# The last block of two down projections as seven quarter products, in a two-layer transformer kernel

## The chip, the core and the metric

The kernel runs on one core of a Trainium2 chip. The time is the device time of the program in microseconds (us). The kernel before took 988.21 us, the median of three runs (988.11 to 988.47).

## What is computed

Two transformer layers on 512 tokens of width 1024, in fp32. Layer A mixes tokens with latent attention, layer B with banded attention; behind each stands an MLP with a squared relu, and behind each mixer and each MLP a layer norm:

```python
def _layernorm(x, g, b):
    mu = x.mean(-1, keepdims=True)
    var = jnp.square(x - mu).mean(-1, keepdims=True)
    return (x - mu) * lax.rsqrt(var + LN_EPS) * g + b

def _mlp(x, w_up, w_down):                 # w_up 1024x4096, w_down 4096x1024
    h = jax.nn.relu(x @ w_up)
    return (h * h) @ w_down

# each layer, alpha = sqrt(2):
x = _layernorm(alpha * x + mixer(x), ln_mix_g[l], ln_mix_b[l])
x = _layernorm(alpha * x + _mlp(x, w_up[l], w_down[l]), ln_mlp_g[l], ln_mlp_b[l])
```

## The kernel before

**Products of split numbers.** TensorE (PE) multiplies in a reduced fp32 form, so each operand is split into a high and a low part (`split`, lines 72 to 84: ScalarE, called ACT here, writes the high part on L77; VectorE, called DVE, subtracts it from the source on L81, or GpSimd, called POOL, if the caller says so). A product is three matmuls: high by high, high by low, low by high (`three`, `group`, L105). Weights come by DMA in pieces of 128x1024 (512 KB), are split into tiles `wh` and `wl` (four of each in rotation), and a weight piece is prepared at most four pieces ahead (`weights`, `AHEAD`).

**Seven products for eight.** Hidden width 4096 is worked in four blocks of 1024 (q = 0 to 3). A block of the up projection, and of the down projection, is a product of two matrices cut into 2x2 quarters, and it is made with seven quarter products in place of eight (the scheme of Winograd). They are named U1 to U7 and D1 to D7. The left factors are sums of quarters: D1 takes a11, D2 a12, D4 a22, D5 a21 - a22, D6 a21 - a22 - a11, D3 a12 plus that sum, D7 a11 - a21 (`Factors.sum`, L700 to L708: DVE, 128x1024 each); each factor is then split (`factor`; tiles `fac`, three in rotation). The right factors are sums of weight quarters, and the DMA makes them: after a weight piece has been split for one product, `add_more` (L204) adds another quarter into the same tile `wq` by a DMA on POOL's queue, and the next product splits the sum. Tile `quada` goes through D1, D5, D6 and D4 in this way, `quadb` through D3 and D7; D2 loads its own quarter (`raw`). Each quarter product takes two weight pieces and, for each of two token tiles (t = 0, 1), 12 matmuls of 128x512 into one PSUM bank. So a D step is 24 matmuls.

**The order.** `STEPS` (line 39) is a table of numbers: one row of it per block, in which U' and D' belong to the next block. PE's instructions keep this written order; a scheduler places those of the other engines, ahead of which a few pins (`pe`, `pin`) and "not before" marks (`behind`) stand. Every engine works through its own list in order and waits where an input is missing. `down_` adds each product from its bank to the residual rows x in SBUF with DVE (L638, L641, L792); products D1 and D6 gather in `u2` (L900).

**The last block before.** In the row for q = 2 to 3 stands `LAST_STEPS`: it ends with U'6 U'7 U'4 D4, and the down projection of block q = 3 is not in it. That block is a plain product (`TokMajor`, class `Hidden`): the four quarters of the hidden rows are split as they are, and eight weight pieces are loaded and split. `finish` first makes columns 0 to 511 for all four token tiles (piece by piece), and then columns 512 to 1023 token by token: 24 matmuls for a token, `add_last` (add and statistics, L631), then `layer_norm(t)` (statistics L488, the power on POOL L443, two DVE passes over 128x1024, L494 and L495), while PE goes on with the next token. In layer A the finished rows of tokens t = 0 and 1 are turned over on PE (`turn_tokens`, L507: 8 transposes into the two banks `tr`, split by ACT and DVE into `xth` and `xtl`) behind the matmuls of tokens 1 and 2; tokens 2 and 3 are turned within `begin`, the start of layer B, between its first products. In layer B the last token's columns 512 to 1023 are made in two halves, and `last_norm` ends the kernel: bank `b` gets x times g less the mean by PE with `xg` (L466, L472, L477) for the lower columns, DVE does the rest (L479, L481), and each piece goes out by its own DMA (L482).

**Layer B's mixer.** For heads h = 0 to 15, `scores`, `weigh`, `turn` and `mix` run with fixed leads. POOL scales the weights of a head (`p`, L1451), masks them (`pm`, L1471), splits some weights of w_sq and w_so (L81), and splits the mixed rows of each of the eight head pairs into `oh` and `ol` (in `mix`); that last split stands behind `muls[h + 4]`, the scaling of a later head. `run_steps` interleaves `proj.part`, the products with w_so, which need `oh` and `ol`.

Of the kernel before, what the change touches and what calls it, by code (L numbers as in the profile page):

```python
# [9 lines left out]
F32R = mybir.dt.float32r  # L10
# [5 lines left out]
P = 128  # L16
# [23 lines left out]
FIRST_STEPS, LAST_STEPS = "U'1 U'2 U'5 U'3 U'6 U'7 U'4 D'1 D'2", "U'1 D5 U'2 D3 U'5 D6 D7 U'3 U'6 U'7 U'4 D4"  # L40
# [8 lines left out]
def build(tc, nc, io, out):  # L49
    with ExitStack() as top:  # L50
# [117 lines left out]
        def queue_seven(name, key, chunk):  # L168
# [20 lines left out]
            def grown(a, jp, *more, aside=None):  # L189
                wh, wl = tiles_of_weights(aside)  # L190
                after = None
                if aside and not early:
                    after = state.pop("plain", None)
                elif (key, a, jp, bool(more)) == ("U", "b", 0, True):
                    after = state.get("s4")
                elif (key, a, more) == ("U", "a", (1, 0)):
                    after = state.pop(("s2", jp), None)
                with behind(after):
                    state["last"] = split(
                        wh, wl, flat(half(a, jp)), keep=(a, bool(more)) == ("b", True) and key == "U"  # L200
                    )
# [29 lines left out]
            def alone(jp, aside=None):  # L231
# [3 lines left out]
                with behind(state["plain"] if aside else state.pop("f1", None) if key == "D" else None):  # L235
                    split(wh, wl, raw)
# [12 lines left out]
            def add(n, asides=(None, None)):  # L249
                for jp, aside in enumerate(asides):  # L250
                    make = (lambda jp=jp, aside=aside: of[n](jp, aside)) if aside else (lambda jp=jp: of[n](jp))
                    stream.append((name, make))
                    off_ring.append(aside is not None)
# [4 lines left out]
        def steps_of():  # L258

            rows = [(-1, FIRST_STEPS)] + [(q, STEPS) for q in range(NFF - 2)] + [(NFF - 2, LAST_STEPS)]  # L260
# [23 lines left out]
        def mlp_stream(l):  # L284
# [13 lines left out]
            add |= {("D", q): queue_seven("down", "D", down(q)) for q in range(NFF - 1)}  # L298
# [6 lines left out]
            for c in range(8):  # L305
                queue("down", io["down"][l, (NFF - 1) * 8 + c])
# [153 lines left out]
        def last_tokens(gb):  # L460
# [8 lines left out]
        def last_norm(gb, minus, diag, xg, b):  # L469

            x = xs[NT - 1]
            pe(nc.tensor.matmul(b, ident, xg, start=True, stop=False))  # L472
            mv = sp.tile([P, 2], F32, tag="mv", bufs=4, name=nm("mv"))
            nc.vector.bn_aggr(mv, stats[NT - 1])
            r = rsqrt_of(mv[:, 1:2])
            nc.scalar.activation(diag, minus, AF.Copy, scale=mv[:, 0:1])
            pe(nc.tensor.matmul(b, diag, gb[0][:, 0:512], start=False, stop=True))  # L477
            late = slice(512, D)
            nc.vector.scalar_tensor_tensor(x[:, late], x[:, late], mv[:, 0:1], gb[0][:, late], ALU.subtract, ALU.mult)  # L479
            for c, src in ((late, x[:, late]), (slice(0, 256), b[:, 0:256]), (slice(256, 512), b[:, 256:512])):  # L480
                pin(nc.vector.scalar_tensor_tensor(x[:, c], src, r, gb[1][:, c], ALU.mult, ALU.add))  # L481
                nc.sync.dma_start(out[(NT - 1) * P : NT * P, c], x[:, c])  # L482

        def layer_norm(t, gb, dst):
# [9 lines left out]
            pin(nc.vector.scalar_tensor_tensor(x, x, mv[:, 0:1], gb[0], ALU.subtract, ALU.mult))  # L494
# [26 lines left out]
        class TokMajor:  # L521
# [25 lines left out]
            def finish(self, gb=None, dst=None, early=None, gb_at=None):  # L547
# [9 lines left out]
                if gb is not None:  # L557
# [3 lines left out]
                    for t in range(NT):  # L561
                        end = dst is None and t == NT - 1
                        n = 2 if end else 1
                        if end:
                            parts = last_tokens(gb)
                        for i in range(n):
                            c = slice(i * 512 // n, (i + 1) * 512 // n)
                            b = bank(512 // n)
                            for kp in range(4):
                                self.group(b, t, kp, ws[kp], c)  # L570
                            pinned[0] = early
                            with tc.high_priority():
                                self.evac(t, slice(512 + c.start, 512 + c.stop), b)
                            pinned[0] = False
                        pinned[0] = early
                        with tc.high_priority():
                            if end:
                                last_norm(gb, *parts)
                            else:
                                layer_norm(t, gb, dst)  # L580
                        if early:
                            prepare(early[t])
                        pinned[0] = False
                        if dst is not None and t in (1, 2):
# [40 lines left out]
        def count(t, c):  # L625
# [4 lines left out]
            for i in range(c.start // n, c.stop // n):  # L630
                pin(nc.vector.bn_stats(stats[t][:, i, :], xs[t][:, i * n : (i + 1) * n]))  # L631
# [144 lines left out]
        def mlp(src, gb, dst, mp):  # L776
# [17 lines left out]
            class Block:  # L794
                def __init__(self, q):
# [4 lines left out]
                    self.fac = {}  # L800

# [69 lines left out]
                def factor(self, n, quad=False):  # L871
                    if quad:
                        f = mp.tile([P, 2, 4, 256], F32R, tag="quada", bufs=1, name=nm("fac"))
                    else:
                        f = mp.tile([P, 2, 4, 256], F32R, tag="fac", bufs=3, name=nm("fac"))
                    g = [self.g.get(a) for a in ("a11", "a12", "a21", "a22")]
                    pair = split(f[:, 0], f[:, 1], g[2] if n == 0 else self.down.sum(n, *g))
                    if (self.q, n) == (0, 1):
                        state["f1"] = state["first"] = pair
                    self.fac[n] = f  # L880

                def down_(self, n):
                    w = [weights("down") for _ in range(2)]
                    f = self.fac.pop(n)
                    key = {3: 5}.get(n) or own_bank[n]
                    for t in range(2):
                        tk = slice(t * P, (t + 1) * P)
                        b = self.bank(("D", key), t)
                        for m in range(4):
                            wh, wl = w[m // 2]  # L890
                            c = slice(m % 2 * 512, (m % 2 + 1) * 512)
                            group(
                                b, three(f[:, 0, m, tk], f[:, 1, m, tk], wh[:, c], wl[:, c]),
                                n not in (2, 3, 4) and m == 0, m == 3, skip_group_check=True,
                            )
                        add = add_scaled if self.q == 0 else add_plain
                        if n == 1 and self.q == 0:
                            nc.vector.tensor_copy(u2[t], b)
                        elif n in (1, 6):
                            nc.vector.tensor_add(u2[t], b, u2[t])  # L900
                        elif n == 2:
                            add(t, lows, b)
                        elif n == 5:
                            add(2 + t, highs, b)
                        elif n == 3:
                            add(t, highs, b)
                        elif n == 7:
                            take(2 + t, highs, b)
                        elif n == 4:
                            add(2 + t, lows, b)  # L910
# [5 lines left out]
            for i, (which, q, n) in enumerate(steps):  # L916
                if which == "D":

                    i_q = steps.index(("U", q, {1: 6, 2: 2}.get(n, 4)))
                    i_last = steps.index(("U", q + 1, {2: 2, 3: 2}.get(n, 6))) - 1  # L920

                    at.setdefault(i_q if (q, n) == (0, 1) else max(min(i - 2, i_last), i_q), []).append((q, n))
            for i, (which, q, n) in enumerate(steps):
                if which == "U":
                    blocks[q].up(n)
                else:
                    blocks[q].down_(n)
                    if (q, n) == (NFF - 2, 6):
                        for t in range(2):
                            take(t, highs, u2[t])  # L930
# [734 lines left out]
```

## Time and profile before

| what | value |
|---|---|
| median of three runs | 988.21 us |
| the profiled execution, its own time | 988.92 us |
| its span, first to last instruction | 987.1 us |
| DVE, ACT, POOL busy | 771.0, 545.5, 240.1 us |
| granted clock of TensorE | 1.00 |
| read from HBM, written | 146.41 MB, 4.22 MB |

A row of the timeline gives start and duration in us, engine, source line, operation, output and inputs, shape and count, and in brackets how long the engine had idled before and who released it. A duration reaches over the start of the next instruction where the engine works in a pipeline, so what an instruction costs its engine is the distance from its start to the next one's. PEld is the loading of weights into TensorE, which lies beside the matmuls.

### The profile page before, as it was taken

What the parts mean: (1) busy time and instruction counts of PE and PEld (TensorE: products, weight loads), DVE (VectorE), ACT (ScalarE), POOL (GpSimd) and SP (SyncE); (2) the same over time, 40 slices, a digit from 0 to 9 for tenths busy, and PEclk for the clock granted to TensorE, in tenths of its full rate; (3) what the DMA queues carried; (4) which work ended last, traced back from release to release, by engine and by line L of the source; (5) the groups of instructions that cost most, each with busy time, mean ns of one, the idle gap of its engine ahead of it and who ended that gap; (6) DMA issues with size and microseconds to landing.
All of it is one profiled execution on the core that took longest, in us unless ns stands there. A gap on an engine that the chain in (4) does not pass through costs nothing.

```text
span 987.1 us, 15665 instructions
## 1 busy us (share of the span) xinstructions
PE 979.5 (99%) x6028; PEld 881.6 (89%) x6028; DVE 771.0 (78%) x1279; ACT 545.5 (55%) x842; POOL 240.1 (24%) x207
## 2 busy tenths in 40 slices
PE   9999999999999999999999999999999999999998
PEld 9988888998999999998898988789998998999986
DVE  6589967989778769887587788798885986888756
ACT  5557644467537637646136787436763763764620
POOL 0231101121212211310002898522221122023000
PEclk9999999999999999999999999999999999999999
DMA  7421236389879968973232212628997797898332
GB/s 263 146 89 43 87 128 193 64 215 234 149 177 234 185 133 245 221 128 120 93 108 86 97 65 97 192 44 173 259 183 126 237 201 119 222 261 146 82 128 85
DMA packets 60678, 149.54 MB, mean 151 GB/s; under 512 B 5259, under 2 KB 10300, under 8 KB 60604
## 3 DMA queue, kind: packets, MB, share of 16 engines
q0 software_dynamic: 24320, 58.73, 34.0%
q1 hardware_dynamic: 36140, 89.56, 26.2%
q8 instruction: 47, 0.77, 0.3%
q10 hardware_dynamic: 144, 0.26, 0.1%
q14 instruction: 27, 0.22, 0.1%
HBM read 146.41 MB, written 4.22 MB: 153 GB/s over the span
## 4 chain that ended last, share of the span: by engine, by line
PE 96%; DVE 2%; POOL 1%; ACT 0%; issue 0%; DVEq 0%; POOLq 0%
PE mm L105 88%; PE tr L105 5%; PE tr L1243 1%; PE tr L742 1%; POOL wl L81 1%; DVE mm L1431 0%; PE tr L1467 0%; DVE o L1502 0%; PE tr L507 0%; POOL p L1451 0%; DVE pt L81 0%; POOL ol L81 0%; PE tr L1007 0%; ACT wh L77 0%; DVE mm L1427 0%
## 5 line engine op out<-in xcount | busy, mean ns | idle before, releaser
L105 PE MATMUL mm<-wh,fac 128*128 128x512 f32 (+1 forms) x944 | 292.7, 386 | 0.0
L77 ACT ACTIVATE wh<-wq 128x1024 fp32r<-128x1024 f32 x164 | 173.9, 1062 | 184.3 <-PE mm L105 137.0
L81 DVE TENSOR_TENSOR wl<-wq,wh 128x1024 fp32r<-128x1024 f32 x164 | 199.4, 1221 | 68.3 <-ACT wh L77 67.5
L105 PE MATMUL mm<-xth,wh 128*128 128x256 f32 (+1 forms) x928 | 243.4, 290 | 0.0
L105 PE MATMUL mm<-xth,wl 128*128 128x256 f32 (+1 forms) x800 | 233.3, 292 | 0.0
L105 PEld LDWEIGHTS mm<-wh,fac 128*128 128x128 f32 x944 | 176.2, 188 | 35.5 <-DVE fac L81 0.6
L105 PE MATMUL mm<-xtl,wh 128*128 128x256 f32 (+1 forms) x672 | 197.1, 293 | 0.0
L105 PE MATMUL mm<-wl,fac 128*128 128x512 f32 (+1 forms) x472 | 182.3, 386 | 0.0
L105 PEld LDWEIGHTS mm<-xth,wh 128*128 128x128 f32 x928 | 168.6, 192 | 3.1
L105 PEld LDWEIGHTS mm<-xth,wl 128*128 128x128 f32 x800 | 153.2, 192 | 2.7
L105 PEld LDWEIGHTS mm<-xtl,wh 128*128 128x128 f32 x672 | 128.7, 191 | 3.0
L77 ACT ACTIVATE wh<-raw 128x1024 fp32r<-128x1024 f32 (+3 forms) x86 | 85.0, 990 | 78.1 <-PE mm L105 57.1
L204 POOL DMA_DIRECT2D wq<-in_up x64 | 77.6, 1238 | 200.2 <-DVE wl L81 193.0
L105 PEld LDWEIGHTS mm<-wl,fac 128*128 128x128 f32 x472 | 88.8, 188 | 16.6
L81 DVE TENSOR_TENSOR wl<-raw,wh 128x1024 fp32r<-128x1024 f32 (+2 forms) x64 | 74.8, 1178 | 30.8 <-ACT wh L77 30.5
L204 POOL DMA_DIRECT2D wq<-in_down x48 | 42.0, 875 | 189.1 <-DVE wl L81 183.2
L81 POOL TENSOR_TENSOR wl<-raw,wh 128x1024 fp32r<-128x1024 f32 (+2 forms) x22 | 47.0, 2138 | 90.3 <-ACT wh L77 70.3
L105 PE MATMUL mm<-wh,ol 128*128 128x512 f32 x128 | 50.3, 393 | 0.9 <-POOL ol L81 0.9
L105 PE MATMUL mm<-wh,oh 128*128 128x512 f32 x128 | 50.7, 396 | 0.0
L105 PE MATMUL mm<-wl,oh 128*128 128x512 f32 x128 | 50.1, 391 | 0.1
L443 POOL TENSOR_TENSOR rs<-mv,half 128x1 f32<-128x1 f32 x16 | 8.9, 554 | 168.1 <-DVE mv L488 163.3
L641 DVE TENSOR_TENSOR x<-mm,x 128x512 f32<-128x512 f32 (+1 forms) x49 | 32.9, 675 | 14.8 <-PE mm L105 14.8
(246 smaller groups left out, 1788.5 us busy)
## 6 DMA issues: line engine op xcount, KB each, us to landing
wq<-in_up POOLq DMA_DIRECT2D x64, 512.0 KB, 7.3
wq<-in_down POOLq DMA_DIRECT2D x48, 512.0 KB, 7.3
wq<-in_up SPq DMA_DIRECT2D x32, 512.0 KB, 6.6
raw<-in_down SPq DMA_DIRECT2D x28, 512.0 KB, 6.1
wq<-in_down SPq DMA_DIRECT2D x24, 512.0 KB, 5.5
raw<-in_up SPq DMA_DIRECT2D x16, 512.0 KB, 4.7
raw<-in_w_o SPq DMA_DIRECT2D x8, 512.0 KB, 3.3
raw<-in_w_sq SPq DMA_DIRECT2D x8, 512.0 KB, 3.3
```

Source lines behind the costliest of these rows:

```text
L77: high = nc.scalar.activation(dst_h, src, AF.Copy)
L81: low = (engine or nc.vector).tensor_sub(dst_l, src, f32(dst_h))
L105: pe(nc.tensor.matmul(dst, st, mv, start=first and i == 0, stop=last and i == len(pairs) - 1, **kw))
L204: state["added", key, a, more, jp] = nc.gpsimd.dma_start(half(a, jp), chunk(*more, jp), accum_op=ALU.add)
L443: state["rs"] = nc.gpsimd.tensor_tensor(r, v, half, ALU.pow)
L641: nc.vector.tensor_add(xs[t][:, c], b, xs[t][:, c])
L742: pe(nc.tensor.transpose(pt[:, a, :], xs[t][:, k * P : (k + 1) * P], ident))
L1243: pe(nc.tensor.transpose(pt[:, kb * P : (kb + 1) * P], p[:, kb * P : (kb + 1) * P], ident))
```

## The change

Block q = 3 of both down projections gets the seven products too. `STEPS` now also serves the row from q = 2 to 3 (so D4 of block 2 stands ahead of U'6, and D'1 D'2 follow U'4), and a last row "D5 D3 D6 D7 D4" follows. `TokMajor` and class `Hidden` are no longer used there, the eight plain weight pieces are no longer loaded, and `u2` is no longer taken apart at the end of block 2.

What becomes of the products of the last block stands in a new function, `last_out`. D1 adds to `u2`; D2 adds to x (columns 0 to 511, with statistics), and then ACT writes `u2` into D2's bank, on which D6 and then D7 go on summing; D5 and D3 go to x as before. D6 completes columns 512 to 1023 of tokens 0 and 1: DVE takes the bank from x, and `layer_norm` of these tokens stands right there. Behind D7, `u2` and D7 go to tokens 2 and 3, and ACT copies columns 0 to 511 of these tokens into new banks, on which D4 sums. So these columns are never written back to x before the norm: `layer_norm` reads them from the bank (`lows`). D4's two weight pieces get their low parts from POOL. Weight splits of this block stand behind the splits of factors (`state["last", ...]`).

In layer A tokens 0 and 1 are turned behind D7 and between the two halves of D4. In layer B D4 of token 3 is made in two banks of 256 columns; token 2's second pass of the norm is a scale on ACT and additions on POOL and DVE (`state["rest"]`), and `last_norm` is laid out over DVE, ACT and POOL, with six output DMAs in place of four behind token 1.

In layer B's mixer, ACT's eviction `low` of the second bank stands behind the sink exponential of a later head; the split of the mixed rows of head pairs m = 5, 6 and 7 goes to DVE, and only m < 5 waits for `muls[h + 4]`.

**DVE, layer A, the end of the last block.** `x_1598`, `x_1600`, `x_1602` and `x_1604` are the rows of tokens 0 to 3; `mm_4826` and `mm_4840` are the banks of D6 and D7, `fac_5043` is D4's factor. Before, where the norm of token 0 is made (`mm_4988` and `mm_5021` are tokens' own banks):

```order
L641 TENSOR_TENSOR x_1598<-mm_4988,x_1598 128x512
L631 BN_STATS bn_4936<-x_1598 128x6
L488 BN_AGGR mv_5015<-bn_4936 128x2
L494 SCALAR_TENSOR_TENSOR x_1598<-x_1598,mv_5015,gb_4890 128x1024
L495 SCALAR_TENSOR_TENSOR x_1598<-x_1598,rs_5017,gb_4890 128x1024
L641 TENSOR_TENSOR x_1600<-mm_5021,x_1600 128x512
L631 BN_STATS bn_4946<-x_1600 128x6
L81 TENSOR_TENSOR xtl_1829<-tr_5054,xth_1827 128x4x128
```

Now, in the same place:

```order
L81 TENSOR_TENSOR wl_4996<-wq_4864,wh_4995 128x1024
L81 TENSOR_TENSOR fac_5043<-a_778_4783,fac_5043 128x1024
L804 TENSOR_TENSOR x_1598<-x_1598,mm_4826 128x512
L804 TENSOR_TENSOR x_1600<-x_1600,mm_4840 128x512
L642 BN_STATS bn_4884<-x_1598 128x6
L642 BN_STATS bn_4901<-x_1600 128x6
L505 BN_AGGR mv_5017<-bn_4884 128x2
L505 BN_AGGR mv_5037<-bn_4901 128x2
L512 SCALAR_TENSOR_TENSOR x_1598<-x_1598,mv_5017,gb_4905 128x1024
L512 SCALAR_TENSOR_TENSOR x_1600<-x_1600,mv_5037,gb_4905 128x1024
L653 TENSOR_TENSOR x_1602<-mm_4826,x_1602 128x512
L804 TENSOR_TENSOR x_1602<-x_1602,mm_4826 128x512
```

The norms of tokens 0 and 1 now stand together, behind the splits for D7 and D4 and ahead of the additions of D7.

**PE, layer A, the turning of token 0.** Before, the last row of token 1's products, the transposes, and the first of token 2's (`fac_4820`):

```order
L105 MATMUL mm_5021<-wl_4972,fac_4817 128x512
L105 MATMUL mm_5021<-wh_4971,fac_4817 128x512
L507 MATMUL tr_5054<-ident,x_1598 128x128 x4
L507 MATMUL tr_5061<-ident,x_1598 128x128 x4
L105 MATMUL mm_5068<-wh_4861,fac_4820 128x512
```

Now D7's last rows (`fac_4991`), the transposes, and D4's first (`fac_5043`):

```order
L105 MATMUL mm_4840<-wl_4996,fac_4991 128x512
L105 MATMUL mm_4840<-wh_4995,fac_4991 128x512
L530 MATMUL tr_5093<-ident,x_1598 128x128 x4
L530 MATMUL tr_5100<-ident,x_1598 128x128 x4
L105 MATMUL mm_5069<-wh_4999,fac_5043 128x512
```

The transposes of token 0 were one token's products (24 matmuls) behind its last sum; now they follow D7 at once, and D4 stands behind them.

**POOL, the end of layer A's MLP.** Before, after the last additions to up weights, the four powers of the norms:

```order
L204 DMA wq_4083<-in_up 128x2x512 x2
L443 TENSOR_TENSOR rs_5017<-mv_5015,half 128x1
L443 TENSOR_TENSOR rs_5050<-mv_5048,half 128x1
L443 TENSOR_TENSOR rs_5097<-mv_5095,half 128x1
L443 TENSOR_TENSOR rs_5145<-mv_5143,half 128x1
```

Now (`wl_5000` and `wl_5047` are the low parts of D4's weights):

```order
L209 DMA wq_4083<-in_up 128x2x512 x2
L209 DMA wq_4682<-in_down 128x1024 x4
L209 DMA wq_4864<-in_down 128x1024 x2
L209 DMA wq_4682<-in_down 128x1024 x2
L81 TENSOR_TENSOR wl_5000<-wq_4682,wh_4999 128x1024
L81 TENSOR_TENSOR wl_5047<-wq_4682,wh_5046 128x1024
L449 TENSOR_TENSOR rs_5019<-mv_5017,half 128x1
L449 TENSOR_TENSOR rs_5039<-mv_5037,half 128x1
```

Eight adding DMAs and two splits of 128x1024 now stand ahead of the first power.

The diff, cut to its core:

```diff
-FIRST_STEPS, LAST_STEPS = "U'1 U'2 U'5 U'3 U'6 U'7 U'4 D'1 D'2", "U'1 D5 U'2 D3 U'5 D6 D7 U'3 U'6 U'7 U'4 D4"
+FIRST_STEPS, LAST_STEPS = "U'1 U'2 U'5 U'3 U'6 U'7 U'4 D'1 D'2", "D5 D3 D6 D7 D4"
...
+                if last:
+                    after = state.pop(("last", state["product"], jp), None)
+                    if state["product"] == 4:
+                        low = nc.gpsimd
...
-            for c in range(8):
-                queue("down", io["down"][l, (NFF - 1) * 8 + c])
...
-            nc.gpsimd.tensor_mul(xg, xs[NT - 1][:, 0:512], gb[0][:, 0:512])
-            return minus, diag, xg, bank()
+            nc.gpsimd.tensor_mul(xg, xs[NT - 1][:, 512:D], gb[0][:, 512:D])
+            return minus, diag, xg, [bank(256) for _ in range(2)]
...
+            t, before, b1 = state["rest"]
+            for c, engine in ((slice(0, 512), nc.gpsimd), (slice(512, D), nc.vector)):
+                engine.tensor_add(before[:, c], before[:, c], b1[:, c])
+                nc.sync.dma_start(out[t * P : (t + 1) * P, c], before[:, c])
             nc.scalar.activation(diag, minus, AF.Copy, scale=mv[:, 0:1])
...
+            for c, to in zip((early, late), b):
+                pe(nc.tensor.matmul(to, diag, gb[0][:, c], start=False, stop=True))
+            for i, src in enumerate(lows):
+                c = slice(i * 256, i * 256 + 256)
+                pin(nc.vector.scalar_tensor_tensor(x[:, c], src[:, 0:256], mv[:, 0:1], gb[0][:, c], ALU.subtract, ALU.mult))
+            nc.scalar.activation(x[:, early], b[0], AF.Copy, scale=r)
+            nc.gpsimd.tensor_add(x[:, early], x[:, early], gb[1][:, early])
+            for c, src in ((lows_, x[:, lows_]), (late, b[1])):
                 pin(nc.vector.scalar_tensor_tensor(x[:, c], src, r, gb[1][:, c], ALU.mult, ALU.add))
                 nc.sync.dma_start(out[(NT - 1) * P : NT * P, c], x[:, c])
+            nc.scalar.dma_start(out[(NT - 1) * P : NT * P, early], x[:, early])
...
+                def last_out(self, n, t, b):
+                    if n == 1:
+                        nc.vector.tensor_add(u2[t], b, u2[t])
+                    elif n == 2:
+                        add_last(t, lows, b)
+                        nc.scalar.activation(b, u2[t], AF.Copy)
...
+                    elif n == 6:
+                        with tc.high_priority():
+                            take(t, highs, b)
+                            count(t, highs)
+                            layer_norm(t, self.gb, dst)
+                    elif n == 7:
+                        add_plain(2 + t, lows, b)
+                        n_banks = 2 if dst is None and t == 1 else 1
+                        self.seeded[t] = bs = [bank() for _ in range(n_banks)]
+                        for i, to in enumerate(bs):
+                            cols = slice(i * 512 // n_banks, (i + 1) * 512 // n_banks)
+                            nc.scalar.activation(to[:, 0 : cols.stop - cols.start], xs[2 + t][:, cols], AF.Copy)
+                        take(2 + t, highs, b)
+                        count(2 + t, highs)
+                        if dst is not None and t == 1:
+                            with tc.high_priority():
+                                dst.turn(0)
+                    elif n == 4:
...
+                            layer_norm(2 + t, self.gb, dst, b)
+                            if dst is not None and t == 0:
+                                dst.turn(1)
...
-            TokMajor(Hidden(), add_last, "down").finish(gb, dst, dst and (0, 0, 0, 1), 1)
...
-                    nc.scalar.activation(low, parts[hi], AF.Copy)
+                    with behind((sinks[min(h + 4, SQH - 1)],) if n2 else None):
+                        nc.scalar.activation(low, parts[hi], AF.Copy)
...
-                state["open"] = (muls[min(h + 4, SQH - 1)],)
-                split(oh[m // 4][:, m % 4, :], ol[m // 4][:, m % 4, :], o.rearrange("p a b -> p (a b)"), nc.gpsimd)
+                if m < 5:
+                    state["open"] = (muls[h + 4],)
+                split(oh[m // 4][:, m % 4, :], ol[m // 4][:, m % 4, :], o.rearrange("p a b -> p (a b)"), nc.gpsimd if m < 5 else None)
```

More of the change, by code (lines that the diff above doesn't have):

```diff
@@ L561, in finish @@
                     for t in range(NT):
[L562 to L575, printed above, removed]
-                        with tc.high_priority():
[L577 to L582, printed above, removed]
+                        b = bank()
+                        for kp in range(4):
+                            self.group(b, t, kp, ws[kp])
+                        pinned[0] = True
+                        with tc.high_priority():
+                            self.evac(t, slice(512, D), b)
+                        with tc.high_priority():
+                            layer_norm(t, gb, dst)
+                        prepare(early[t])
                         pinned[0] = False
-                        if dst is not None and t in (1, 2):
+                        if t in (1, 2):
                             with tc.high_priority():
@@ L868, in up_out, with factor @@
                             nc.scalar.activation(self.g[done], self.g[done], AF.Square)
[L871 to L875, printed above, removed]
+                def factor(self, n):
+                    f = mp.tile([P, 2, 4, 256], F32R, tag="fac", bufs=3, name=nm("fac"))
                     g = [self.g.get(a) for a in ("a11", "a12", "a21", "a22")]
-                    pair = split(f[:, 0], f[:, 1], g[2] if n == 0 else self.down.sum(n, *g))
+                    pair = split(f[:, 0], f[:, 1], self.down.sum(n, *g))
                     if (self.q, n) == (0, 1):
                         state["f1"] = state["first"] = pair
+                    if self.q == NFF - 1:
+                        if n == 3:
+                            state["fac3"] = pair
+                        for jp in range(2):
+                            state["last", {5: 3, 3: 6, 6: 7, 7: 4}.get(n), jp] = pair
                     self.fac[n] = f
@@ L884, in down_ @@
                     f = self.fac.pop(n)
-                    key = {3: 5}.get(n) or own_bank[n]
+                    last = self.q == NFF - 1
+                    key = {3: 5}.get(n) or (1 if last and n in (6, 7) else own_bank[n])
+                    seeded = n in (2, 3, 4) or last and n in (6, 7)
                     for t in range(2):
                         tk = slice(t * P, (t + 1) * P)
[L888 to L910, printed above, removed]
@@ new lines, in down_ @@
+                        bs = self.seeded[t] if last and n == 4 else [self.bank(("D", key), t)]
+                        if len(bs) > 1:
+                            parts = last_tokens(self.gb)
+                        for i, b in enumerate(bs):
+                            cols = slice(i * 512 // len(bs), (i + 1) * 512 // len(bs))
+                            for m in range(4):
+                                wh, wl = w[m // 2]
+                                c = slice(m % 2 * 512 + cols.start, m % 2 * 512 + cols.stop)
+                                group(
+                                    b[:, 0 : cols.stop - cols.start],
+                                    three(f[:, 0, m, tk], f[:, 1, m, tk], wh[:, c], wl[:, c]),
+                                    not seeded and m == 0, m == 3, skip_group_check=True,
+                                )
+                            if len(bs) > 1:
+                                pinned[0] = True
+                                with tc.high_priority():
+                                    count(2 + t, cols, b[:, 0:256])
+                                pinned[0] = False
```

104 lines of the change are left out of this document (66 added, 38 removed).

## The prediction

> **What bounds the kernel now.** I read the page first: the busy times, then the chain of work that ended last.
>
> ```profile
> span 987.1 us, 15665 instructions
> PE 979.5 (99%) x6028; PEld 881.6 (89%) x6028; DVE 771.0 (78%) x1279; ACT 545.5 (55%) x842; POOL 240.1 (24%) x207
> PE 96%; DVE 2%; POOL 1%; ACT 0%; issue 0%; DVEq 0%; POOLq 0%
> ```
>
> PE is 96% of the chain, so fewer matmuls ought to be time won. But 78% for DVE is an average, so next come the windows: the end of each MLP (from the last matmul of U4), and, as a picture of a stretch of quarter products, block 2 of layer A from its U4 on. The columns are the stretch, its length, busy time of PE, weight loading, DVE, ACT and POOL, the clock, the DMA share, GB/s.
>
> ```profile
> 454.87:505.82 50.95, 50.95 (x234) 42.12 (x233) 33.62 (x47) 15.86 (x18) 1.66 (x3) 1.00 0.30 104
> 930.62:980.29 49.67, 49.67 (x243) 41.91 (x242) 32.40 (x44) 12.29 (x13) 2.94 (x4) 1.00 0.30 109
> 381.83:409.71 27.88, 27.88 (x170) 25.02 (x169) 26.38 (x27) 18.91 (x21) 5.92 (x6) 1.00 0.95 247
> ```
>
> In the ends as they are DVE works 33.62 of 50.95 us: one third is free. In the third stretch, which the last block will now resemble, DVE works 26.38 of 27.88 us (95%). So the question is not how many matmuls go, but whether DVE, with more work and less time, lets PE have them.
>
> **The matmuls removed.** The marks on PE's timeline, with the prices:
>
> ```profile
> 381.83 0.40 PE L105 MATMUL mm<-wh,fac 128*128 128x512 f32 x1
> ...
> 454.87 0.40 PE L105 MATMUL mm<-wh,fac 128*128 128x512 f32 x1
> ...
> 505.82 0.28 PE L105 MATMUL mm<-xth,wh 128*128 128x256 f32 x1
> ...
> 899.65 0.39 PE L105 MATMUL mm<-wl,fac 128*128 128x512 f32 x1
> 900.33 0.39 PE L105 MATMUL mm<-wl,fac 128*128 128x512 f32 x1
> ...
> 930.62 0.40 PE L105 MATMUL mm<-wh,fac 128*128 128x512 f32 x1
> ...
> 974.45 0.28 PE L105 MATMUL mm<-wl,fac 128*128 128x256 f32 x1
> 974.81 0.28 PE L105 MATMUL mm<-wl,fac 128*128 128x256 f32 x1
> ```
>
> Every third matmul reads `wl`: 0.68 us from 899.65 to 900.33, so 0.227 for 128x512, and 0.36 / 3 = 0.12 for 128x256. A D step of 24 costs 24 x 0.227 = 5.45. Seven steps for eight removes 36 matmuls of 128x512 and 24 of 128x256 in all: 8.2 + 2.9 = 11.1 us. That is the most that PE can give.
>
> **DVE, layer A.** The order of DVE now, from D1's first bank on, is that of block 2, where this stretch can be read:
>
> ```profile
> 385.28 0.68 DVE L900 TENSOR_TENSOR u<-mm,u 128x512 f32<-128x512 f32 x1
> ...
> 388.11 2.35 DVE L81 TENSOR_TENSOR wl<-wq,wh 128x1024 fp32r<-128x1024 f32 x2
> 390.38 1.22 DVE L81 TENSOR_TENSOR fac<-uv,fac 128x1024 fp32r<-128x1024 f32 x1
> 391.51 0.68 DVE L641 TENSOR_TENSOR x<-mm,x 128x512 f32<-128x512 f32 x1
> 392.11 1.21 DVE L703 TENSOR_TENSOR uv<-uv,a 128x1024 f32<-128x1024 f32 x1
> ...
> 480.47 1.28 DVE L631 BATCH_NORM_STATS2 bn<-x 128x6 f32<-128x512 f32 x2
> ...
> 976.24 1.31 DVE L494 SCALAR_TENSOR_TENSOR x<-x,mv,gb 128x1024 f32<-128x1024 f32 x1
> 977.47 0.41 DVE L641 TENSOR_TENSOR x<-mm,x 128x256 f32<-128x256 f32 x1
> 977.80 1.27 DVE L495 SCALAR_TENSOR_TENSOR x<-x,rs,gb 128x1024 f32<-128x1024 f32 x1
> 979.00 0.41 DVE L631 BATCH_NORM_STATS2 bn<-x 128x6 f32<-128x256 f32 x1
> ```
>
> By distance from start to start, a 128x1024 of two inputs costs 1.135 (2.27 for two), a 128x512 0.60, a statistic of 512 about 0.6, of 256 about 0.37 (0.41 less the overlap), a norm pass over 1024 1.2. D1's first reading stands 385.28 - 381.83 = 3.45 behind U4's last matmul. From there on DVE has, up to the second `xtl` split of token 0, which frees the banks `tr` for token 1: ten weight splits (two for layer B), four sums and five factor splits of 128x1024, 19 x 1.135 = 21.6; sixteen of 128x512, 9.6; five statistics, 3.0; four small ones, 0.5; four norm passes, 4.8. With 0.5 for waits (0.29 stood there in block 2) that is 40.0. Then come the last transposes of token 1 (0.4) and D4's second half, 12 x 0.227 = 2.7. Layer B's first product would start 3.45 + 40.0 + 0.4 + 2.7 = 46.6 behind U4. Before, D4 of block 2 stood behind U4; now it is ahead of it, so the old distance is 505.82 - 454.87 - 5.45 = 45.5. Layer A: **+1.1**, where the matmuls promised -5.5. PE's own work in it is 7 x 5.45 + 2 x 0.8 (transposes, estimated at 8 of 0.1) = 39.8; it waits some 7 us, mostly ahead of the two turnings.
>
> Two orders cost nothing by this sum: D4 now ahead of U'6 is the same work in another place, and ACT, with 15.86 of 50.95 us used, holds the added copies into banks.
>
> **DVE, layer B.** The same way to the kernel's last instruction:
>
> ```profile
> 981.21 0.26 DVE L474 BATCH_NORM_AGGREGATE mv<-bn 128x2 f32<-128x24 f32 x1
> 981.51 0.78 DVE L479 SCALAR_TENSOR_TENSOR x<-x,mv,gb 128x512 f32<-128x512 f32 x1
> 982.39 0.75 DVE L481 SCALAR_TENSOR_TENSOR x<-x,rs,gb 128x512 f32<-128x512 f32 x1
> 983.13 0.88 DVE L481 SCALAR_TENSOR_TENSOR x<-mm,rs,gb 128x256 f32<-128x256 f32 x2
> ```
>
> 17 x 1.135 = 19.3; fifteen of 128x512, 9.0; six statistics of 512, 3.6, four of 256, 1.5; eight small, 1.2; four passes of 1024, 4.8, three of 512 at 0.74, 2.2, three of 256, 1.2; together 42.8, with 0.7 for waits 43.5. Behind U4: 47.0. U4 ends 5.45 later than before, at 936.07, so DVE ends at 983.1; before it ended at 983.13 + 0.88 = 984.0. Layer B: **-0.9**. Six output pieces in place of four: the last one starts with the last pass as before, and I cost the change at nothing; were two issues of a queue in its way, a microsecond.
>
> **The two orders in layer B's mixer.**
>
> ```profile
> 605.69 0.25 ACT L1447 ACTIVATE mm<-nb,sink 128x4 f32<-128x4 f32 x1
> ...
> 607.83 0.44 PE L1467 MATMUL tr<-ident,p 128*128 128x128 f32 x2 [0.75 <-POOL p L1451]
> 618.09 0.50 PE L105 MATMUL mm<-wh,ol 128*128 128x512 f32 x1 [0.86 <-POOL ol L81]
> ```
>
> PE waits 0.75 and 0.86 us for POOL here; the `ol` splits of m = 5 to 7 leave POOL for DVE, which frees POOL for `p`. I take **-1.2** (bounds -1.6, both gone, and +0.5, if `low` behind two sinks of 0.25 is what PE waits for).
>
> **POOL beside DVE.** D4's two weight splits go to POOL, and at the end half of token 2's last addition. What POOL and DVE do to each other:
>
> ```profile
> 616.76 1.27 POOL L81 TENSOR_TENSOR ol<-o,oh 128x512 fp32r<-128x512 f32 x1
> ...
> 628.37 1.73 POOL L81 TENSOR_TENSOR ol<-o,oh 128x512 fp32r<-128x512 f32 x1 [3.37 <-ACT oh L77]
> ...
> 631.57 2.39 POOL L81 TENSOR_TENSOR wl<-raw,wh 128x1024 fp32r<-128x1024 f32 x1
> ```
>
> ```profile
> 629.27 1.91 DVE L81 TENSOR_TENSOR wl<-raw,wh 128x1024 fp32r<-128x1024 f32 x1 [0.33 <-ACT wh L77]
> ...
> 632.42 2.62 DVE L81 TENSOR_TENSOR w_fac<-wq,w_fac 128x1024 fp32r<-128x1024 f32 x1
> ```
>
> ```profile
> 976.28 0.55 POOL L443 TENSOR_TENSOR rs<-mv,half 128x1 f32<-128x1 f32 x1 [4.89 <-DVE mv L488]
> ```
>
> DVE's split at 632.42 took 2.62 in place of 1.22, and could only finish about 1.1 us behind POOL's (631.57 + 2.39): it stood still meanwhile. So two splits on POOL, 2 x 2.39 = 4.8 us, cost DVE what it cannot fill with other kinds. Where they fall (D4's weights), DVE has two x -= bank, two statistics and two aggregates, 2.8 us, and the four norm passes, 4.8. Is a norm pass, with both big inputs in SBUF, blocked too? POOL's power at 976.28 ran 0.55 us in the middle of the pass begun at 976.24, which kept its 1.31: no sign of it, though it is only 128x1. I take the passes as free: no loss in the MLP ends, and 0.4 at the kernel's end, where DVE's and POOL's additions to token 2 meet (from 0 to 0.9).
>
> [...]
>
> **Sum.** 1.1 - 0.9 - 1.2 + 0.4 = -0.6 against the profiled execution's 988.92, so 988.3; the median lies 0.7 below it: **987.6**. About 0.2% (2 us) is what a measurement can tell from no change.
>
> **The cases.**
>
> *No change: DVE gives back what PE saves (987.6; 0.45).* Bounds of the terms: mixer -0.4 or +1.7, DVE waits +-1.5 in all, collision +-0.5, so 985 to 990. Inside it, 0.15 for faster, 0.26 same, 0.04 slower.
>
> *POOL's splits stop DVE's norm passes (slower, 0.26).* Of 4.8 us only 2.8 are covered: +2.0 in each layer, as DVE is the bound there, so 991.6. For it: both inputs of the pass are big and in SBUF, as in the rows that did block. Against: the power's row. It decides once the splits fall among the passes; earlier they meet factor splits, and cost as much. With bounds 989 to 994; 0.02 of it same.
>
> *PE's saving arrives (faster, 0.16).* If DVE's list is shorter in time than I add up, or its splits run ahead of D1, the ends go by PE: A 39.8 in place of 45.5, B 7 x 5.45 + 3.7 of tail = 41.9 in place of 984.0 - 936.07 = 47.9: -11.7, with the mixer 975.3 (972 to 982, the upper end where PE still waits for half of the DVE excess). Against: 26.38 busy of 27.88 in the same list.
>
> *The adding DMA is late (slower, 0.13).* D4's second piece is summed by a DMA that starts when D6's split has read the tile. Of the adding transfers in block 2:
>
> ```profile
> DMA to landing us min/median/max: 5.4/8.0/15.3
> ```
>
> By the list above that is 19.9 us behind 385.28 on block 2's clock, 405.2; landing at +8.0, then ACT 1.1 and POOL 2.4, is 416.7. D4 needs it at about 420.8 (turning over, half a product done): 4.1 us of cover. At 15.3 it would be 3.2 late in A and, without a turning over in the way, about 4 in B: some +7.5 in all, 995.1 (992 to 997). Against: in the second half of an end few other DMAs are left (share 0.30 in the windows above, 0.95 in block 2).
>
> The range 980 to 994.5 leaves out most of the third case (0.12) and some 0.08 of the fourth. Faster by over 0.2%: 0.15 + 0.16 = 0.31; same 0.26 + 0.02 = 0.28; slower 0.04 + 0.24 + 0.13 = 0.41.
>
> **What would show it.** In the new profile: DVE over 90% busy from U4 to the end of each MLP, PE idle some 7 us in layer A's, with DVE named as releaser (`x`, `fac`, `xtl`), norm passes of 1.3 us beside POOL's 2.4 us splits (first case), or passes of 2 us or more (second); D4's first matmul waiting for `wl` from POOL (fourth); PE over 97% busy in the ends (third). The mixer's 0.75 and 0.86 gone. If U4 to layer B's start takes under 44 us, my sum of DVE's list is wrong.

## The result, and the profile after

The changed kernel takes 994.15 us (median of four runs, 993.72 to 994.38) against 988.34 of before on the same chip: a ratio of 1.0057, 95% interval 1.0045 to 1.0069. It is slower, where the prediction put no change (987.6) first. The profiled execution took 993.72 us against 988.92, 4.8 us more, and its span is 4.8 us longer as well, so the span can be taken apart.

The page of the changed kernel: the span, the busy times, and the engines of the chain that ended last.

```profile
span 991.9 us, 15685 instructions
PE 970.2 (98%) x5972; PEld 871.3 (88%) x5972; DVE 800.7 (81%) x1306; ACT 569.3 (57%) x871; POOL 265.3 (27%) x226
PE 88%; DVE 8%; issue 2%; POOL 1%; ACT 0%; POOLq 0%; DVEq 0%
```

PE lost 9.3 us of work and the kernel became longer; 8% of the chain now lies on DVE, against 2% before. The two ends, in the windows from D1's first matmul on (columns as in the prediction): in layer A to layer B's first product, in layer B to DVE's last instruction.

```profile
459.61:508.09 48.48, 41.33 (x186) 32.80 (x185) 48.14 (x60) 27.09 (x31) 13.26 (x11) 1.00 0.51 115
937.86:987.12 49.26, 41.84 (x190) 33.03 (x188) 48.57 (x64) 23.79 (x28) 17.70 (x15) 1.00 0.46 98
```

DVE is busy 48.14 of 48.48 us and 48.57 of 49.26, where before it was 33.62 of 50.95. PE works 41.33 of 48.48. (The prediction calls the marks at 454.87, 381.83 and 930.62 U4's last matmul. They read `fac`: each is the first matmul right behind U4, at 381.83 that of D1, at 454.87 and 930.62 that of block 2's D4. Its distances hold as they are.)

PE's waits in layer A's end and at layer B's start, and the marks:

```profile
459.61 0.40 PE L105 MATMUL mm<-wh,fac 128*128 128x512 f32 x1
...
498.46 1.06 PE L530 MATMUL tr<-ident,x 128*128 128x128 f32 x8 [3.01 <-DVE x L518]
...
504.23 1.25 PE L530 MATMUL tr<-ident,x 128*128 128x128 f32 x8 [1.95 <-DVE xtl L81]
...
508.09 0.28 PE L105 MATMUL mm<-xth,wh 128*128 128x256 f32 x1
...
515.66 0.38 PE L105 MATMUL mm<-wl,xth 128*128 128x256 f32 x1 [0.67 <-DVE wl L81]
...
647.67 0.27 PE L754 MATMUL tr<-ident,x 128*128 128x128 f32 x1
...
937.86 0.40 PE L105 MATMUL mm<-wh,fac 128*128 128x512 f32 x1
```

From these and the rows of before, the 4.8 us by stretches. The last two are read from DVE's end (984.01 before, 987.12 after) and the span's.

| stretch | before | after | difference |
|---|---|---|---|
| start to D1 of layer A's last block (before: 454.87 + 5.45 for D4's new place) | 460.32 | 459.61 | -0.7 |
| from there to layer B's first product | 45.50 | 48.48 | +3.0 |
| layer B's mixer, to the turning over behind it (before: 505.82 to 645.88) | 140.06 | 139.58 | -0.5 |
| from there to D1 of layer B's last block (before with the same 5.45) | 290.19 | 290.19 | 0.0 |
| from there to DVE's last instruction | 47.94 | 49.26 | +1.3 |
| from there to the end of the span | 3.09 | 4.78 | +1.7 |

Now the place where the prediction was to be decided: the first norm passes of layer A's last block. DVE, then POOL, in the changed kernel:

```profile
490.14 1.28 DVE L642 BATCH_NORM_STATS2 bn<-x 128x6 f32<-128x512 f32 x2
491.34 0.32 DVE L505 BATCH_NORM_AGGREGATE mv<-bn 128x2 f32<-128x12 f32 x2
491.58 3.15 DVE L512 SCALAR_TENSOR_TENSOR x<-x,mv,gb 128x1024 f32<-128x1024 f32 x1
494.65 1.27 DVE L512 SCALAR_TENSOR_TENSOR x<-x,mv,gb 128x1024 f32<-128x1024 f32 x1
```

```profile
491.26 2.39 POOL L81 TENSOR_TENSOR wl<-wq,wh 128x1024 fp32r<-128x1024 f32 x1
493.61 1.54 POOL L449 TENSOR_TENSOR rs<-mv,half 128x1 f32<-128x1 f32 x1
495.13 1.21 POOL L449 TENSOR_TENSOR rs<-mv,half 128x1 f32<-128x1 f32 x1
```

The pass that begins while POOL splits D4's second weight piece takes 3.15 us, its twin right behind it 1.27. The long one ends 1.1 us behind POOL's end (491.26 + 2.39 = 493.65), as the DVE split of 2.62 us did in the kernel before. And the powers, 0.55 us elsewhere, take 1.54 and 1.21 beside the passes: they wait too. Beside POOL's first split (488.79 to 491.26) two `x -= bank` took 1.27 us together and two statistics 1.28, no longer than elsewhere. In layer B the two passes take 4.33 us together in place of 2.4.

### The profile page after: what moved, and what is told of

It reads as the page before. It is cut to its first block, busy times and chain, and to the rows that moved or that the text cites. A ratio compares the mean times of both kernels' runs of the same rounds, so it can differ in the third digit from the quotient of the medians.

```text
span 991.9 us, 15685 instructions
## 1 busy us (share of the span) xinstructions
PE 970.2 (98%) x5972; PEld 871.3 (88%) x5972; DVE 800.7 (81%) x1306; ACT 569.3 (57%) x871; POOL 265.3 (27%) x226
## 4 chain that ended last, share of the span: by engine, by line
PE 88%; DVE 8%; issue 2%; POOL 1%; ACT 0%; POOLq 0%; DVEq 0%
PE mm L105 80%; PE tr L105 5%; DVE wl L81 1%; DVE x L512 1%; DVE fac L81 1%; DVE bn L642 1%; PE tr L1296 1%; DVE x L653 1%; PE tr L754 1%; POOL wl L81 1%; DVE x L518 1%; DVE x L804 0%; PE tr L1520 0%; DVE mm L1484 0%; DVE o L1556 0%
## 5 line engine op out<-in xcount | busy, mean ns | idle before, releaser
L77 ACT ACTIVATE wh<-wq 128x1024 fp32r<-128x1024 f32 x188 | 199.1, 1060 | 204.7 <-PE mm L105 159.0
L105 PE MATMUL mm<-wh,fac 128*128 128x512 f32 (+1 forms) x904 | 284.3, 389 | 6.5 <-ACT mm L972 2.1
L81 DVE TENSOR_TENSOR wl<-wq,wh 128x1024 fp32r<-128x1024 f32 x184 | 223.4, 1220 | 79.2 <-ACT wh L77 78.5
L105 PEld LDWEIGHTS mm<-wh,fac 128*128 128x128 f32 x904 | 169.2, 188 | 43.5 <-ACT mm L972 2.9
L105 PE MATMUL mm<-wl,fac 128*128 128x512 f32 (+1 forms) x452 | 175.4, 388 | 0.0
L209 POOL DMA_DIRECT2D wq<-in_down x64 | 55.8, 872 | 262.1 <-DVE wl L81 259.6
L77 ACT ACTIVATE wh<-raw 128x1024 fp32r<-128x1024 f32 (+3 forms) x74 | 72.1, 977 | 45.6 <-PE mm L105 38.2
L81 DVE TENSOR_TENSOR wl<-raw,wh 128x1024 fp32r<-128x1024 f32 (+3 forms) x52 | 59.4, 1156 | 8.7 <-ACT wh L77 7.7
L105 PE MATMUL mm<-wh,ol 128*128 128x512 f32 x128 | 50.2, 392 | 0.0
L81 DVE TENSOR_TENSOR fac<-uv,fac 128x1024 fp32r<-128x1024 f32 x32 | 38.9, 1217 | 0.4 <-ACT fac L77 0.4
L77 ACT ACTIVATE fac<-uv 128x1024 fp32r<-128x1024 f32 x32 | 33.4, 1049 | 10.2 <-DVE uv L717 4.5
```

The costliest lines, as they stand in the source:

```text
L77: high = nc.scalar.activation(dst_h, src, AF.Copy)
L81: low = (engine or nc.vector).tensor_sub(dst_l, src, f32(dst_h))
L105: pe(nc.tensor.matmul(dst, st, mv, start=first and i == 0, stop=last and i == len(pairs) - 1, **kw))
L209: state["added", key, a, more, jp] = nc.gpsimd.dma_start(half(a, jp), chunk(*more, jp), accum_op=ALU.add)
```

## The experiments

All are timed in five rounds against the kernel before on the same chip (988.25 to 988.49 there). The changed kernel was not timed again beside them, so a difference from its 994.15 is one between separate rounds; the kernel before moved by 0.15 us at most between those (988.34 beside the changed kernel).

**POOL's splits taken away.** In `split`, for D4's weights of the last block:

```diff
+                if engine == "zero":
+                    low = nc.scalar.activation(dst_l, src, AF.Copy, scale=0.0)
...
-                        low = nc.gpsimd
+                        low = "zero"
```

> The changed kernel, but the low parts of D4's weights (two pieces per layer, last block) are not subtracted by POOL: ACT writes zeros in their place, so the low-order product of these weights is left out. Standstill theory (a POOL instruction that reads SBUF and a DVE instruction with two SBUF inputs exclude each other, norm passes too): the first norm pass of 3.15 us falls to about 1.3 in both layers, 1.9 us less each, about 990.3 us against 994.15. Rival, the pass is slow for another reason (two long passes in a row, its inputs from a late transfer): the pass stays at 3 us and the time at 994. Rival, DVE's list is longer than it was added up, standstill or not: 994 as well, with other rows longer.

Measured: 990.89 us, ratio 1.0028 (1.0017 to 1.004), 3.3 less than the changed kernel. The passes fall to 1.2 each:

```profile
491.16 0.34 DVE L508 BATCH_NORM_AGGREGATE mv<-bn 128x2 f32<-128x12 f32 x2
491.42 2.46 DVE L515 SCALAR_TENSOR_TENSOR x<-x,mv,gb 128x1024 f32<-128x1024 f32 x2
```

So it is POOL's split that stops them; both rivals fall. In layer B the end is 47.4 us long in place of 49.26, -1.9 as the standstill theory says. In layer A the two turnings over come 1.9 earlier too, but layer B's first product only 0.3. The reason stands in PE's row and the windows of this run:

```profile
502.18 1.30 PE L533 MATMUL tr<-ident,x 128*128 128x128 f32 x8 [1.95 <-DVE xtl L84]
...
507.62 0.28 PE L108 MATMUL mm<-xth,wh 128*128 128x256 f32 x1
```

```profile
502.00:504.00 2.00, 1.82 (x10) 1.55 (x11) 2.00 (x6) 1.08 (x2) 0.00 (x0) 0.81 0.73 231
504.00:506.00 2.00, 2.00 (x6) 1.52 (x6) 1.96 (x5) 0.12 (x1) 0.55 (x1) 0.50 0.08 31
506.00:508.00 2.00, 2.00 (x11) 1.64 (x10) 1.00 (x3) 1.06 (x1) 0.00 (x0) 0.83 0.00 0
```

Behind PE's second wait the granted clock was 0.81, 0.50 and 0.83, and D4's twelve matmuls took 4.4 us in place of 2.85. Most of what DVE won in layer A was lost to a slower PE. So for layer A the 1.9 us of standstill are read from the two turnings over; that the time falls with them is seen in layer B alone.

**The splits given to DVE.** The edit:

```diff
-                        low = nc.gpsimd
+                        low = None
```

> The changed kernel with the low parts of D4's weights made by DVE instead of POOL, nothing left out. Standstill theory: DVE gains two rows of 1.135 per layer and loses 1.95 of standing still, +0.3 per layer, about 994.8 us. If POOL's split costs DVE nothing: +2.27 per layer, about 998.7. If DVE has room and only POOL's lateness counts: 990 or less.

Measured: 998.19 us, ratio 1.0101 (1.0086 to 1.0116), 4.0 above the changed kernel. Neither figure was met outright: near 998.7, but not for its reason. In layer A token 0's second pass, on which PE waits, came behind three more rows for tokens 2 and 3 and two splits of layer B's weights, since the scheduler laid DVE's list out anew. PE waited 7.66 us, and its clock fell again:

```profile
503.08 1.94 PE L530 MATMUL tr<-ident,x 128*128 128x128 f32 x8 [7.66 <-DVE x L518]
```

```profile
500.00:502.00 2.00, 0.00 (x0) 0.00 (x0) 2.00 (x4) 0.60 (x1) 0.00 (x0) 0.50 0.01 4
502.00:504.00 2.00, 0.92 (x5) 0.95 (x6) 2.00 (x2) 0.00 (x0) 0.00 (x0) 0.50 0.59 184
```

The transposes took 1.94 us in place of 1.06, and layer A's end 53.6 us. In layer B, where DVE's order changed too, the end took 50.2 us, 1.0 more than in the changed kernel. So this run says that DVE has no room for two more rows, not what the standstill alone is worth.

**DVE relieved.** In the last block the low parts of the weights of D5, D3, D6 and D7 aren't made; the matmuls read the high parts in their place:

```diff
...
+                    if state["product"] != 4:
+                        with behind(after):
+                            high = nc.scalar.activation(wh, flat(half(a, jp)), AF.Copy)
+                        state["last"] = (high, high)
+                        wl = wh
...
```

> The changed kernel with the low parts of the weights of D5, D3, D6 and D7 in the last block left out: the matmuls that read them read the high parts instead, so PE's work is the same and DVE loses eight rows of 1.135 us (9.1 us) per layer. If DVE's list sets the ends: layer A from D1's first matmul to layer B's first product falls from 48.5 to 41 to 43 us (PE's own work there is 39.8), layer B's end alike by 6 to 7; in all about 981 us (979 to 984). If PE, ACT or a transfer sets them: 992 to 994.

Measured: 986.87 us, ratio 0.9986 (0.9977 to 0.9995): 7.3 below the changed kernel with PE's work untouched, so DVE's list does set the ends; but half of what was expected. Layer A's end fell from 48.48 to 46.42, layer B's from 49.26 to 45.2. PE came to token 0's turning over without a wait, and then stood:

```profile
460.12 0.40 PE L105 MATMUL mm<-wh,fac 128*128 128x512 f32 x1
...
492.79 1.03 PE L536 MATMUL tr<-ident,x 128*128 128x128 f32 x8
...
501.21 1.71 PE L536 MATMUL tr<-ident,x 128*128 128x128 f32 x8 [4.12 <-DVE xtl L81]
...
506.54 0.28 PE L105 MATMUL mm<-xth,wh 128*128 128x256 f32 x1
```

What DVE has to do behind D6 and D7 (additions, statistics, norms, splits for layer B), with POOL's splits still beside it, does not shrink when rows in front of it go. That stretch keeps PE waiting 4.12 us, and the clock fell here too (0.59 from 501 to 504), which cost D4's twelve matmuls behind it another 1.1 us (3.97 in place of 2.85).

**PE relieved.** Of the three matmuls of a product, that with the weights' low part is left out in D5 and D3:

```diff
-   three(f[:, 0, m, tk], f[:, 1, m, tk], wh[:, c], wl[:, c]),
+   three(f[:, 0, m, tk], f[:, 1, m, tk], wh[:, c], wl[:, c])[:: 2 if last and n in (5, 3) else 1],
```

> The changed kernel with one of the three matmuls of each product (the low parts of the weights) left out in D5 and D3 of the last block: PE loses 16 matmuls, 3.6 us, per layer; DVE's work is the same, though its order shifts a little behind D6 in layer A, so layer B's end is the clean reading. If DVE's list sets the end: layer B from D1's first matmul to DVE's last instruction stays at 49.3 us (to 0.5), the whole 993 to 995. If PE sets it: 3.6 us less per layer, 987.

Measured: 994.72 us, ratio 1.0062 (1.0049 to 1.0075). Layer B's end, from D1's first matmul to DVE's last instruction:

```profile
938.84 0.40 PE L105 MATMUL mm<-wh,fac 128*128 128x512 f32 x1
...
956.08 0.50 PE L105 MATMUL mm<-wh,fac 128*128 128x512 f32 x1 [2.54 <-ACT fac L77]
```

```profile
987.65 0.47 DVE L497 SCALAR_TENSOR_TENSOR x<-mm,rs,gb 128x256 f32<-128x256 f32 x1
```

988.12 - 938.84 = 49.28 us, against 49.26, with 16 matmuls (3.6 us) fewer. PE only waited longer, as at 956.08 (0.73 us at this place in the changed kernel): its work is not what sets this end.

**The last piece from SP's queue.**

```diff
-            nc.scalar.dma_start(out[(NT - 1) * P : NT * P, early], x[:, early])
+            nc.sync.dma_start(out[(NT - 1) * P : NT * P, early], x[:, early])
```

> The changed kernel with the last output piece issued from SP's queue, as all others, instead of ACT's. The span ended 4.6 us behind the last issue, before 3.1. If the second queue costs this at the program's end: about 1.5 us less, 992.7. If it is the transfer or the lateness of POOL's last addition: 994.1, unchanged to 0.3.

Measured: 993.99 us, ratio 1.006 (1.0048 to 1.0073): no change. It isn't the second queue.

**Token 2's output issued earlier.**

```diff
-                nc.sync.dma_start(out[t * P : (t + 1) * P, c], before[:, c])
...
+                for c in (slice(0, 512), slice(512, D)):
+                    nc.sync.dma_start(out[t * P : (t + 1) * P, c], xs[0][:, c])
```

> The changed kernel with token 2's two output pieces at the end read from token 0's finished rows, and so issued some 5 us earlier (the rows of tokens 2 are then token 0's); all sums are still made. If the end waits for 1 MB of output that goes out together (0.5 MB before): the distance from the last issue to the end of the span falls from 4.6 to about 3.1 us, about 992.6. If not: 994.1.

Measured: 993.96 us, ratio 1.0058 (1.0045 to 1.007): no change either, so the bytes that go out together are not it.

**Layer B's end without late work on POOL.**

```diff
-            for c, engine in ((slice(0, 512), nc.gpsimd), (slice(512, D), nc.vector)):
+            for c, engine in ((slice(0, 512), nc.vector), (slice(512, D), nc.vector)):
...
-            nc.scalar.activation(x[:, early], b[0], AF.Copy, scale=r)
-            nc.gpsimd.tensor_add(x[:, early], x[:, early], gb[1][:, early])
-            for c, src in ((lows_, x[:, lows_]), (late, b[1])):
+            for c, src in ((lows_, x[:, lows_]), (early, b[0]), (late, b[1])):
...
-            nc.scalar.dma_start(out[(NT - 1) * P : NT * P, early], x[:, early])
```

> The changed kernel with POOL's two late additions at layer B's end (token 2's lower half, a 256-wide piece of token 3) and ACT's scaling of that piece given to DVE, all outputs from SP's queue; nothing left out. DVE gains two rows (0.60 and 0.35) and loses 0.43 of standing beside POOL: its last instruction moves from 987.1 to about 987.6. If late work on POOL, or the end of its queue, makes the 4.6 us between the last issue and the span's end (3.1 before): the distance falls to 3.1, the whole to about 992.7. If it doesn't: 994.6.

Measured: 992.65 us, ratio 1.0043 (1.0031 to 1.0056), 1.5 below the changed kernel. The last DVE row of the changed kernel, POOL's and ACT's, then the last DVE row of this one:

```profile
986.65 0.47 DVE L497 SCALAR_TENSOR_TENSOR x<-mm,rs,gb 128x256 f32<-128x256 f32 x1
```

```profile
986.14 1.17 POOL L495 TENSOR_TENSOR x<-x,gb 128x256 f32<-128x256 f32 x1
```

```profile
987.34 0.35 ACTq L499 DMA_DIRECT2D out<-x  x1
```

```profile
span 991.6 us, 15683 instructions
```

```profile
987.65 0.74 DVE L495 SCALAR_TENSOR_TENSOR x<-x,rs,gb 128x512 f32<-128x512 f32 x1
```

From DVE's end (988.39) to the span's end (991.6) it is now 3.2 us, against 4.78 in the changed kernel and 3.09 before. So the two additions that POOL ends with (and ACT's scaling ahead of one) lengthen what follows DVE's end by about 1.6 us. That they end later than DVE explains 0.2 of it (987.31 against 987.12). The rest lies behind the last issue.

The closing instructions of the queues, which stand at one line, show where. Their columns are count, duration in ns (least, median, most), first and last start in us. A DRAIN stands near the end of POOL's queue and of SP's, in SP's behind its waits for the output transfers. In the changed kernel, in the kernel before, and in this run:

```profile
L1716 POOLq DRAIN  x1: 5497/5497/5497, 985.7 to 985.7; - x1
L1716 SPq DRAIN  x2: 7/7/7, 990.3 to 990.3; - x2
```

```profile
L1661 POOLq DRAIN  x1: 3257/3257/3257, 981.5 to 981.5; - x1
L1661 SPq DRAIN  x2: 7/7/7, 986.2 to 986.3; - x2
```

```profile
L1713 POOLq DRAIN  x1: 4436/4436/4436, 984.8 to 984.8; - x1
L1713 SPq DRAIN  x2: 7/7/7, 990.8 to 990.8; - x2
```

In the changed kernel POOL's DRAIN ends at 991.2 (985.7 + 5.5), 3.9 us behind its last addition and 0.9 behind SP's, and the span ends 0.7 later. Before it ended at 984.8, ahead of SP's 986.2, and in this run at 989.2, ahead of 990.8. So POOL's queue is now the last to close, which is about half of the 1.7 us. The other half is SP's: its DRAIN comes 3.2 us behind DVE's end, against 2.2 before and 2.4 in this run. In the two runs before this one it comes 3.1 behind, so neither the second queue nor the bunching makes it. Why POOL's DRAIN takes so long, and why SP's comes later with POOL's late work, stays open.

**The mixer's orders alone, in the kernel before**, both, and the split alone:

```diff
...
-                    nc.scalar.activation(low, parts[hi], AF.Copy)
+                    with behind((sinks[min(h + 4, SQH - 1)],) if n2 else None):
+                        nc.scalar.activation(low, parts[hi], AF.Copy)
...
-                state["open"] = (muls[min(h + 4, SQH - 1)],)
+                if m < 5:
+                    state["open"] = (muls[h + 4],)
...
```

> The kernel before with the two small orders of layer B's mixer alone (low behind a later sink, the split of head pairs 5 to 7 on DVE). From the traces (mixer from layer B's first product behind its start to the first turning over, 1.2 us shorter): 987.1 against 988.3 of before. Rival, the two waits only came and went with the different clock of the end of layer A: 988.3.

> The kernel before with one of the mixer's two orders alone: the split of head pairs 5 to 7 on DVE; ACT's eviction low stays where it was. If the split carries the gain, as the two waits for POOL (0.75 and 0.86 us) say: 987.2 against 988.3. If low behind the later sink carries it: 988.3. If each has a share: about 987.8.

Measured: 987.17 us (ratio 0.999, 0.9982 to 0.9999) and 987.79 (0.9993, 0.9984 to 1.0002). PE's waits in the first, and in the second:

```profile
607.30 0.66 PE L1467 MATMUL tr<-ident,p 128*128 128x128 f32 x4 [0.40 <-POOL p L1451]
```

```profile
607.40 0.66 PE L1467 MATMUL tr<-ident,p 128*128 128x128 f32 x4 [0.76 <-POOL p L1451]
616.97 0.50 PE L105 MATMUL mm<-wh,ol 128*128 128x512 f32 x1 [0.18 <-DVE ol L81]
```

The split on DVE takes 0.86 to 0.18, the later `low` takes 0.76 to 0.40: each has a share, about 0.7 and 0.3 us by the two traces' mixers (139.34 and 139.02 against 140.06), though by the times the split alone cannot be told from no change. The two orders without the rest are 0.1% faster than the kernel before, with the interval just clear of one, and 0.7% faster than the changed kernel.

## Why the prediction was wrong, point by point

**The step that failed** is in "POOL beside DVE": "I take the passes as free: no loss in the MLP ends". The row behind it, POOL's power of 0.55 us at 976.28 beside a pass begun at 976.24, was read as a power in the middle of a pass. The two start 0.04 us apart, released by the same `mv`, and such a pair can go either way. The run with DVE relieved shows it, in layer A and in layer B (DVE's pass, then POOL's power):

```profile
487.03 1.28 DVE L518 SCALAR_TENSOR_TENSOR x<-x,mv,gb 128x1024 f32<-128x1024 f32 x1
...
962.57 1.31 DVE L518 SCALAR_TENSOR_TENSOR x<-x,mv,gb 128x1024 f32<-128x1024 f32 x1
```

```profile
487.08 1.66 POOL L455 TENSOR_TENSOR rs<-mv,half 128x1 f32<-128x1 f32 x1 [8.15 <-DVE mv L511]
...
962.62 0.56 POOL L455 TENSOR_TENSOR rs<-mv,half 128x1 f32<-128x1 f32 x1 [8.15 <-DVE mv L511]
```

Begun 0.05 us behind its pass, the power took 1.66 us in A and 0.56 in B; what decides between the two isn't shown. In the kernel before all sixteen powers of the norms start 0.04 to 0.06 us behind a pass or 0.4 ahead of one, and all took 0.55 to 0.57: that trace had no power begun in the middle of a pass and couldn't settle it. Here powers that came while a pass ran took 1.54 and 1.21. So a short instruction that starts with a long one says nothing on whether the long one blocks. The row that was nearest in shape, the DVE split of 2.62 us, had it right. Cost: 1.95 us in layer A, 1.9 in layer B. The second case ("POOL's splits stop DVE's norm passes", 991.6) names the mechanism and its price of 2.0 per layer, and had 0.26; the passes of 3.15 and 1.27 us bear it out.

**DVE's list as the bound** was right, and so were its sums. Layer A: 40.0 us from D1's first reading to token 0's second `xtl`; measured 41.6 (463.06 to 504.69), 39.7 without the standstill. Layer B: 43.5; measured 45.8 (941.31 to 987.12), and 43.5 without 1.9 of standstill and the 0.43 that a pass of 512 lost beside POOL's addition (1.17 us for 0.74; the prediction put 0.4 there). PE's waits in layer A's end are 48.48 - 41.33 = 7.15, "some 7" foretold.

**"I cost the change at nothing"** of the output was the second wrong term: 1.7 us, by POOL's late additions and the closing of its queue, not by the issues that the prediction had in mind.

**Layer B's start** was not in the sum. DVE comes to it late, with splits for its weights behind the norms: PE waits 0.67 us at 515.66, and from the first product to the first matmul behind the last turning over (519.31 against 516.29) the start is 0.75 longer.

**The mixer**: -1.2 foretold. Its stretch is 0.5 shorter, with 0.75 of later start in it, so -1.2; alone it brought 1.1.

**PE's saving arrives** was refuted; the run with DVE relieved shows that even 9.1 us less of DVE per layer brings back only 2.1 and 4.0. **The late adding DMA** didn't come: in the changed kernel these transfers land in a median of 5.3 us in layer A's end (below) and 5.5 in layer B's, at most 6.8, where block 2's went up to 15.3:

```profile
DMA to landing us min/median/max: 5.1/5.3/6.7
```

**The start**, 0.7 us earlier, is there before any instruction that the change touches, and the runs above scatter by as much (D1 at 459.31 to 460.19); it is not the change's.

In sum, from -0.6: +1.9 of standstill in layer A; +1.8 in layer B beside the 0.4 foretold; +1.7 at the end; +0.75 at layer B's start; -0.7 at the beginning: 4.8, what the profile shows, with none left over beyond a tenth.

## What to carry to other kernels

Before counting matmuls saved, add up the list of the engine that feeds them over the same stretch, row by row; here the list foretold the two ends to a few tenths, once the standstill is taken out. Work moved to POOL was not free for DVE here (1.9 us per layer), though with the splits left to DVE, and another order of its list, the kernel took 998.19 us: look for what DVE does beside it, and take as evidence only rows of the same size whose starts lie well apart. A part of a change that is good by itself (here the mixer's two orders) is worth timing alone, before it disappears in the loss of the rest.

## What the runs showed of the hardware

A stretch in which PE waited could cost more than the wait. The granted clock fell to 0.50 behind a wait of 1.95 us in the run with POOL's splits taken away (an earlier one there was some 1.1 us: the 3.01 of the changed kernel less the 1.9 won), to 0.59 behind one of 4.12 with DVE relieved, and to 0.50 during one of 7.66 with the splits on DVE. D4's twelve matmuls behind the first two took 4.4 and 3.97 us in place of 2.85, the transposes behind the third 1.94 in place of 1.06. In the changed kernel's profiled execution the clock stayed at 1.00 behind waits of 3.01 and 1.95. A slower PE didn't always cost time: in the run with token 2's output issued earlier, whose layer A is that of the changed kernel, the matmuls from 499.77 to 502.75 us, behind a wait of 2.99, stood 0.43 us apart in place of 0.227, and PE only waited 0.35 ahead of token 1's turning in place of 1.95. How long a wait has to be for the clock to fall isn't shown: 1.95 us went both ways.

In these traces POOL's instructions and DVE's norm passes held each other up both ways: a pass took 3.15 us in place of 1.27 beside POOL's split, and three powers 1.21 to 1.66 in place of 0.55 beside a pass.
